# Mixer of a hybrid decoder layer: TensorE in program order with level steps woven into projections, and modulation columns summed by rows

## The chip, the cores and the metric

The kernel runs on one core of one Trainium2 chip. The metric is the time of one execution on the device in microseconds (us); the kernel before takes 2466.71 us, the median of three runs (2466.24 to 2473.23). The engines are TensorE (PE in the rows; PEld is its weight load), VectorE (DVE), ScalarE (ACT), GpSimd (POOL) and SyncE (SP, which issues most DMAs).

## What is computed

One layer for one sequence of T = 2048 tokens and D = 1024 channels, in float32:

```python
mod = silu(c) @ ada_w + ada_b                      # 6 x 1024 columns: shift, scale, gate, twice
h = rms_norm(x, mix_norm_g) * (1 + scale_m) + shift_m
proj = h @ w_in + b_in
q_a, k_a, v_a, q_h, f_h, i_h, g_h = split(proj)    # 512, 128, 128, 512, 512, 512, 512 columns
attn = rms_norm(window_attention(q_a, k_a, v_a, sinks), attn_out_g)
f = lb + (1 - lb) * sigmoid(f_h)                   # recurrence, 4 heads of 128:
#   S_t = diag(f_t) S_(t-1) + (1 - f_t) i_t^T ;  o_t = S_t^T silu(q_h)_t
rec = rms_norm(o, hgrn_out_g) * silu(g_h)
x = x + gate_m * (concat(attn, rec) @ w_out)
# then a gated MLP with a causal convolution of width 3 and the second shift, scale and gate, and a last rms_norm
```

The first half, up to `w_out`, is the mixer; the change lies in it.

## The kernel before, in words

**Tiling.** The mixer works through four groups `g` of 512 tokens (`GT`), each of four blocks of 128. A group's normalised input lies as two float32r parts, `hhi` and `hlo`, by eight slices `k` of 128 channels. Weights are loaded (`..r`), and split into a high part (`..h`, on ACT) and a low part (`..l`, on DVE or POOL). A projection is 24 matmuls into one PSUM bank: for each `k` high by high, low by high and high by low (`mm3`, line 187). The program's names: `hq`, `hf` are the recurrence's query and forget logits of a head, `ps_i` its values (192 matmuls of 256 columns, two weight halves `i 0` and `i 1`), `qp`/`ps_q`, `k`, `v` the attention's, `hg` the output gate.

**The recurrence** goes by heads in pairs (0,1) and (2,3). `hg_q` and `hg_f` evict the projections (`a_q`, `f`, and `K` = 1 - f). `hg_scores` (line 781) prepares both heads on DVE (products `raw`, split into `ph` on ACT and `pl` on POOL; `a_q` and `K` scaled by running products `tot`), and then does ten **level** matmuls (names `lv`, w = 4 to 64, both heads in turn), each reading `a_q` and `K`. After each level `scaled` updates `a_q` and `K` for the next, and DVE puts the result into the score tile `AT` by a predicated copy (ACT does so for w = 32 and 64). Six **sums** with a matrix of ones follow (`lv_d`, 1 and 2, three of each head; the last takes two copies), and two transposes `ktp` of K. `hg_state` (line 886) makes the state (`U`, `mid`, `car`) and the outputs `ho`.

**PSUM banks** are in pools: `mm` 3 (projections), `hg` 2 (levels, sums, ktp, U, ho), `at` 2, `tp` 1. A matmul waits until the bank it is to fill has been emptied.

**Order.** A scheduler orders each engine's instructions unless the engine is pinned to program order (lines 36 to 63). In the mixer's main loop (lines 935 to 984) only ACT is pinned, in parts; TensorE and DVE are placed by the scheduler.

```python
            weights(g, "i", 0, ahead=1)
            pin(True, S)
            hg_scores((0, 1))
            i_tok = proj_i()
            hg_state((0, 1))
```

**Modulation.** 40 column blocks of the modulation are made, of which 24 (16 to 39) are deferred into the group loop: `after()` (line 592) does one at six places of each group through `mod_part` (line 207): one load of 1024 x 128 (512 KB), one multiply by the condition over 128 x 1024, and three additions that halve it. There is one buffer (`ada`, bufs=1). After four blocks `mod_cols_of` sums over partitions with TensorE.

Of the kernel before, what the change touches and what calls it, by code (L numbers as in the profile page):

```python
# [53 lines left out]
def kernel(ctx, tc, x, c, ada_w, ada_b, mix_norm_g, w_in, b_in, attn_sinks, attn_out_g,  # L54
# [175 lines left out]
    with ExitStack() as mx:  # L230
# [103 lines left out]
        for g in range(NG):  # L334
# [254 lines left out]
        for g in range(NG):  # L589
            hhi, hlo = hh  # L590

            def after():

                if defer:
                    t = defer.pop(0)
                    if t % 4 == 0:
# [10 lines left out]
            def proj_i():  # L607
                i_tok = mt.tile([P, BPG, 512], F32, tag="i_tok", bufs=1, name=f"itok_{g}")
                for pp in range(2):
                    ws = weights(g, "i", pp)  # L610
                    for bp in range(2):
                        ps = bank(f"ps_i{g}_{pp}_{bp}", "mm").rearrange("p (a b) -> p a b", a=2)
                        for bb in range(2):
                            b = 2 * bp + bb
                            bs = slice(b * P, (b + 1) * P)
                            for k in range(KT):
                                wh, wl = (t[:, k % 4, :] for t in ws[k // 4])
                                mm3(ps[:, bb, :], hhi[:, k, bs], hlo[:, k, bs], wh, wl, k == 0, k == KT - 1)
                        cs = slice(pp * 256, (pp + 1) * 256)
                        V.tensor_tensor(out=i_tok[:, 2 * bp:2 * bp + 2, cs], in0=ps,  # L620
                                        in1=bi_bc[:, cs].unsqueeze(1).broadcast_to([P, 2, 256]), op=ALU.add)
                return i_tok

            def proj_attn():


                ps = proj(weights(g, "k", 0), f"ps_k{g}")
# [14 lines left out]
                qT = []  # L642
                for pp in range(2):
                    ws = weights(g, "qp", pp)
                    for jj in range(2):
                        j = 2 * pp + jj
                        ps = proj(ws[jj], f"ps_q{g}_{j}")
                        pair = [qa.tile([P, GT], F32R, tag=f"q{j}{e}", name=f"q_{g}_{j}{e}") for e in range(2)]
                        for e in range(2):
                            hp = slice(e * 64, e * 64 + 64)  # L650
                            S.activation(pair[e][hp, :], ps[hp, :], AF.Identity, bias=col("qb", j)[hp, :])
# [913 lines left out]
```

## Time and profile before

| | us |
|---|---|
| median of three runs | 2466.71 (2466.24 to 2473.23) |
| the profiled execution | 2456.9 |
| its span, first to last instruction | 2455.1 |
| TensorE busy (11521 matmul records) | 2296.7, 94% |
| VectorE busy | 1903.9, 78% |
| ScalarE busy | 971.7, 40% |
| GpSimd busy | 917.9, 37% |
| mean granted TensorE clock | 0.973 |

The mixer takes the first 960 us or so of the span, the output projection and the MLP the rest. The busy shares are means over both; the rows below are read by stretches. In a row of the timeline the figure in brackets is the idle time of that engine just before the instruction, with what ended it. A matmul's duration holds the engine's whole pipeline, so from start to start it is shorter than the duration shown. The granted clock is given as a share of the upper level of 2.4 GHz; 0.50 is the lower level of 1.2 GHz.

### The profile page before, as it was taken

The page shows a single profiled execution, that of the slowest core. Times are in us where ns is not written, and L with a number is a line of the kernel's source. Part 1 is how long each engine was busy: PE and PEld are TensorE (multiplying, and loading weights), DVE is VectorE, ACT ScalarE, POOL GpSimd, SP SyncE. Part 2 cuts the span into 40 slices and gives each one's busy share as a digit, 9 for nine tenths or more (in the row PEclk, how much of TensorE's full clock was granted, in tenths as well). Part 3 has the DMA queues.
Part 4 walks back from the last instruction along what each step waited for, and adds up shares of the span by engine and source line. Part 5 has one row for each costly group of instructions (what it writes and reads, how often), then busy time and mean ns, then how long its engine had stood idle before and what let it go on. Part 6 is the DMA issues. An engine that isn't in the chain of part 4 may idle for free.

```text
span 2455.1 us, 31438 instructions
## 1 busy us (share of the span) xinstructions
PE 2296.7 (94%) x11521; PEld 1908.9 (78%) x11521; DVE 1903.9 (78%) x2737; ACT 971.7 (40%) x1658; POOL 917.9 (37%) x760
## 2 busy tenths in 40 slices
PE   5889898998999899999999999899999988999997
PEld 4777786887778778887888888788888776777886
DVE  8888778888876877468888888877888687676766
ACT  3336523723652364455333333433333243323322
POOL 6222212213221221033665664588888710110000
PEclk8999999999999999999999999999999999999999
DMA  8343223223222238574433444654544587777453
GB/s 216 91 121 91 90 69 112 87 81 101 86 87 61 78 120 269 169 244 142 146 123 122 137 130 133 192 164 154 176 158 143 164 278 205 210 188 210 184 215 116
DMA packets 335445, 359.74 MB, mean 147 GB/s; under 512 B 12405, under 2 KB 279371, under 8 KB 335291
## 3 DMA queue, kind: packets, MB, share of 16 engines
q1 hardware_dynamic: 320315, 301.36, 38.8%
q0 software_dynamic: 14976, 56.37, 8.4%
q8 instruction: 91, 1.49, 0.2%
q14 instruction: 63, 0.52, 0.1%
HBM read 250.19 MB, written 107.49 MB: 146 GB/s over the span
## 4 chain that ended last, share of the span: by engine, by line
PE 66%; DVE 13%; DMA 8%; issue 7%; POOL 3%; ACT 2%; SPq 0%; DVEq 0%; POOLq 0%; ACTq 0%
PE ps_u L46 28%; PE ps_d L46 10%; PE ps_o L46 6%; PE lv L46 3%; PE ps_hg L46 3%; PE ps_hq L46 2%; PE ps_hf L46 2%; PE ps_i L46 2%; PE att_o L46 2%; DVE ada L46 2%; DMA Sp<-in_w_down_dram 2%; DMA ada<-in_ada_w_dram 2%; PE ps_q L46 1%; DVE AT L46 1%; DVE raw L46 1%
## 5 line engine op out<-in xcount | busy, mean ns | idle before, releaser
L46 ACT ACTIVATE Th<-da 128x896 fp32r<-128x896 f32 x88 | 83.9, 953 | 230.7 <-PE ps_d L46 210.7
L46 DVE SCALAR_TENSOR_TENSOR cc<-ub,cols,cc 128x1024 f32<-128x1024 f32 x88 | 153.2, 1741 | 14.2 <-ACT cc L46 12.0
L46 DVE TENSOR_TENSOR Tl<-da,Th 128x896 fp32r<-128x896 f32 x88 | 97.1, 1111 | 73.0 <-ACT Th L46 72.7
L46 PE MATMUL lv<-a_q,K 128*128 128x128 f32 (+2 forms) x768 | 80.3, 265 | 42.1 <-DVE K L46 40.0
L46 POOL DMA_DIRECT2D x_d<-o x32 | 27.2, 858 | 237.0 <-DVE o L46 237.0
L46 PEld LDWEIGHTS lv<-a_q,K 128*128 128x128 f32 (+2 forms) x768 | 71.9, 176 | 54.8 <-DVE K L46 28.5
L46 POOL TENSOR_TENSOR s<-wu_0r,s 128x512 f32<-128x512 f32 x44 | 59.2, 1345 | 107.3 <-DVE ws_0l L46 14.7
L46 DVE TENSOR_TENSOR cc<-cc,v 128x1024 f32<-128x1024 f32 x44 | 63.1, 1433 | 43.4 <-ACT cc L46 43.4
L46 POOL TENSOR_TENSOR s<-wu_1r 128x512 f32<-128x512 f32 x44 | 70.6, 1605 | 69.6 <-DVE t_T4l L46 15.7
L46 POOL MEMSET AT<- 128x512 f32 x16 | 8.5, 533 | 233.2 <-PE ho L46 210.4
L46 ACT ACTIVATE cc<-cc 128x1024 f32<-128x1024 f32 x44 | 46.7, 1061 | 121.3 <-DVE cc L46 121.3
L46 POOL TENSOR_TENSOR wu_1r<-wu_0r,wu_1r 128x512 f32<-128x512 f32 x44 | 92.4, 2099 | 3.1
L46 POOL TENSOR_TENSOR pl<-raw,ph 128x512 fp32r<-128x512 f32 x32 | 44.8, 1401 | 101.2 <-ACT ph L46 101.2
L46 POOL TENSOR_SCALAR rv_d<-ssd 128x2 f32<-128x2 f32 x8 | 5.1, 637 | 184.5 <-ACT dx L46 184.5
L46 POOL TENSOR_TENSOR s<-s,wu_0r 128x512 f32<-128x512 f32 x44 | 73.7, 1674 | 0.0
L46 DVE TENSOR_TENSOR v<-ps_u,v 128x512 f32<-128x512 f32 x88 | 60.4, 686 | 15.5 <-PE ps_u L46 12.0
L46 DVE COPY_PREDICATED AT<-lev,lv 128x512 f32<-128x512 uint32 (+1 forms) x96 | 70.1, 730 | 2.4 <-PE lv L46 1.2
L46 DVE TENSOR_TENSOR ada<-ada,cond 128x1024 f32<-128x1024 f32 (+1 forms) x37 | 52.7, 1424 | 16.4 <-DMA ada<-in_ada_w_dram 16.3
L46 ACT ACTIVATE cc<-ub,cols 128x1024 f32<-128x1024 f32 x44 | 54.6, 1240 | 26.3 <-DVE ub L46 26.3
L46 DVE TENSOR_TENSOR a_q<-a_q,tot 128x256 f32<-128x256 f32 x96 | 52.4, 546 | 12.5 <-PE lv L46 11.5
L46 DVE TENSOR_TENSOR o<-ps_d,u 128x512 f32<-128x512 f32 x72 | 49.2, 684 | 15.4 <-ACT u L46 13.9
L46 DVE TENSOR_TENSOR ub<-ps_u,u 128x512 f32<-128x512 f32 x88 | 60.0, 682 | 0.1
(2114 smaller groups left out, 8561.5 us busy)
## 6 DMA issues: line engine op xcount, KB each, us to landing
da<-act_d SPq DMA_DIRECT2D x88, 448.0 KB, 5.8
wu_0r<-in_w_up_dram SPq DMA_DIRECT2D x44, 512.0 KB, 4.4
wu_1r<-in_w_up_dram SPq DMA_DIRECT2D x44, 512.0 KB, 4.4
act_d<-cc POOLq DMA_DIRECT2D x42, 512.0 KB, 4.2
ada<-in_ada_w_dram SPq DMA_DIRECT2D x40, 512.0 KB, 5.9
x_d<-o POOLq DMA_DIRECT2D x32, 512.0 KB, 6.5
act_d<-sm POOLq DMA_DIRECT2D x21, 768.0 KB, 4.1
x<-in_x_dram SPq DMA_DIRECT2D x26, 512.0 KB, 5.6
```

The source lines that it names most:

```text
L46: ins = fn(*args, **kwargs)
```

## The change

**TensorE's order.** TensorE is pinned with ACT from a group's first `hq` projection to the end of the pair (2,3). The projections become generators that yield after each quarter (six matmuls; twelve of 256 columns in `ps_i`), and `weave` runs one step of a recurrence generator, then one piece of the projections:

```diff
+            def weave(gen, *fill):
+                rest = (i for one in fill for i in one)
+                for _ in gen:
+                    next(rest, None)
+                for _ in rest:
+                    pass
```

`hg_scores` yields after every level, sum and transpose (18 steps); the preparation is taken out of it as `hg_prep(h)`, one head at a time. The body of a group becomes:

```diff
+            pin(True, S, TE)
...
+                run(steps_h(hg_q, 0, "hq"), steps_h(hg_f, 0, "hf"), steps_h(hg_q, 1, "hq"))
+                hg_prep(0)
+                run(steps_h(hg_f, 1, "hf"))
+            hg_prep(1)
+            run(steps_i(0), steps(lambda: weights(g, "k", 0), f"ps_k{g}", take_k))
+            q2 = [] if g == 0 else [steps_h(hg_q, 2, "hq")]
+            weave(hg_scores((0, 1)), steps_i(1), *q2)
+            weave(hg_state((0, 1)), steps_h(hg_f, 2, "hf"))
+            mod_step()
+            hg_prep(2)
+            run(steps_h(hg_q, 3, "hq"), steps_h(hg_f, 3, "hf"))
+            mod_step()
+            hg_prep(3)
+            run(steps_q(0), steps_q(1))
+            mod_step()
+            weave(hg_scores((2, 3)), steps_q(2), steps_q(3))
+            mod_step()
+            weave(hg_state((2, 3)), steps(lambda: weights(g, "v", 0), f"ps_v{g}", take_v))
+            pin(False, S, TE)
```

So `weave` of the levels has 8 pieces (`i 1`) in the first pair of the first group, 12 (`i 1` and `hq` 2) in the other pairs (0,1), and 8 (`q` 2 and 3) in the pairs (2,3). The load of the k weights moves from behind `hf` 3 to between `i 0` and `i 1`.

**Modulation by rows.** The 24 column blocks become 48 steps: a part of 512 columns has eight row blocks of 128 x 512 (256 KB), each multiplied by one scalar per partition and added to the part, with two buffers; one step stands at four places of a group and one in each of the eight units of attention. DVE is not pinned and the steps may run ahead of their place.

```diff
-        V.tensor_tensor(out=raw, in0=raw, in1=cond.unsqueeze(2).broadcast_to([P, KT, P]), op=ALU.mult)
-        for n in (4, 2):
-            V.tensor_tensor(out=raw[:, 0:n, :], in0=raw[:, 0:n, :], in1=raw[:, n:2 * n, :], op=ALU.add)
-        V.tensor_tensor(out=to[:, t % 4, :], in0=raw[:, 0, :], in1=raw[:, 1, :], op=ALU.add)
...
+                raw = mt2.tile([P, 4 * P], F32, tag="ada", bufs=2, name=f"ada_{n}_{k}")
+                SY.dma_start(out=raw, in_=ada_v[:, k, 16 * P + n * 4 * P:16 * P + (n + 1) * 4 * P])
...
+            if k == 0:
+                V.tensor_scalar(out=acc_, in0=raw, scalar1=cond[:, 0:1], scalar2=None, op0=ALU.mult)
+            else:
+                V.scalar_tensor_tensor(out=acc_, in0=raw, scalar=cond[:, k:k + 1], in1=acc_, op0=ALU.mult, op1=ALU.add)
+            if k == KT - 1:
+                mod_cols_of(16 + 4 * n, mpart[0])
```

On DVE the eight steps of the first part stand within the two preparations of the first group, and those of two other parts nearly in a row near the ends of groups 1 and 3.

**What stands where: TensorE at the first pair of group 1.** In the names the first number is the group, then the head, then w; a row that stands for several matmuls ends in x4. Before:

```order
L46 MATMUL ps_i1_0_1_3013<-w1_i_0_1l_2675,hhi_1_2520 128x256
L46 MATMUL lv_1_0_4_2806<-a_q1_0_2625,K_1_0_2664 128x128 x4
L46 MATMUL lv_1_1_4_2816<-a_q1_1_2703,K_1_1_2748 128x128 x4
L46 MATMUL ps_i1_0_1_3013<-w1_i_0_1h_2674,hlo_1_2521 128x256
...
L46 MATMUL ps_i1_0_1_3013<-w1_i_0_0h_2668,hhi_1_2520 128x256
L46 MATMUL lv_1_0_8_2826<-a_q1_0_2625,K_1_0_2664 128x128 x4
L46 MATMUL ps_i1_0_1_3013<-w1_i_0_0l_2669,hhi_1_2520 128x256
...
L46 MATMUL lv_1_1_8_2836<-a_q1_1_2703,K_1_1_2748 128x128 x4
```

After:

```order
L46 MATMUL ps_i1_0_1_2865<-w1_i_0_1h_2677,hlo_1_2523 128x256
L46 MATMUL ps_k1_2921<-hhi_1_2522,w1_k_0h_2741 128x512
...
L46 MATMUL ps_k1_2921<-hhi_1_2522,w1_k_0l_2742 128x512
L46 MATMUL lv_1_0_4_2956<-a_q1_0_2628,K_1_0_2667 128x128 x4
L46 MATMUL ps_i1_1_0_2972<-w1_i_1_0h_2805,hhi_1_2522 128x256
...
L46 MATMUL ps_i1_1_0_2972<-w1_i_1_0h_2805,hlo_1_2523 128x256
L46 MATMUL lv_1_1_4_2985<-a_q1_1_2706,K_1_1_2773 128x128 x4
L46 MATMUL ps_i1_1_0_2972<-w1_i_1_1h_2811,hhi_1_2522 128x256
...
L46 MATMUL ps_i1_1_0_2972<-w1_i_1_1h_2811,hlo_1_2523 128x256
L46 MATMUL lv_1_0_8_3007<-a_q1_0_2628,K_1_0_2667 128x128 x4
```

Before, the levels of both heads stand among single matmuls of `ps_i`'s first half; now the first half and all of `ps_k` stand ahead of the first level, and twelve matmuls of the second half stand between one level and the next.

**ACT in the first group**, from the last query eviction on. Before:

```order
L46 ACTIVATE w0_i_1_1h_749<-w0_i_1_1r_747 128x1024
L46 ACTIVATE ph0_0_0_756<-raw0_0_0_761 128x512
L46 ACTIVATE p1_0_0_760<-raw1_0_0_766 128x256
L46 ACTIVATE ph0_0_1_771<-raw0_0_1_776 128x512
L46 ACTIVATE p1_0_1_775<-raw1_0_1_781 128x256
L46 ACTIVATE ph1_0_0_757<-raw2_0_0_789 128x512
L46 ACTIVATE ph1_0_1_772<-raw2_0_1_797 128x512
L46 ACTIVATE AT_0_0_753<-lv_0_0_32_869 32x4x32 x2
L46 ACTIVATE AT_0_1_754<-lv_0_1_32_884 32x4x32 x2
```

After:

```order
L46 ACTIVATE a_q0_2_767<-ps0_4_198,cols_137 128x512
L46 ACTIVATE s_q0_2_769<-ps0_4_198,cols_137 128x512
L46 ACTIVATE ph0_0_1_774<-raw0_0_1_779 128x512
L46 ACTIVATE p1_0_1_778<-raw1_0_1_784 128x256
L46 ACTIVATE ph1_0_1_775<-raw2_0_1_792 128x512
L46 ACTIVATE w0_k_0h_802<-w0_k_0r_800 128x1024
L46 ACTIVATE w0_i_1_0h_808<-w0_i_1_0r_806 128x1024
L46 ACTIVATE w0_i_1_1h_814<-w0_i_1_1r_812 128x1024
...
L46 ACTIVATE kd0_703<-ps_k0_924,cols_137 64x512 x2
```

Before, a weight half of `i` is split ahead of the preparations' splits and k's weights come much later; now k's weights are split behind `ph1` of head 1, and k's own evictions (kd) follow.

**TensorE at the end of pair (2,3) in group 1**: sums and transposes. Before (between the rows shown stand matmuls of `ps_q`):

```order
L46 MATMUL lv_1_2_d_3598<-ph0_1_2_3435,ones_r_694 128x512
L46 MATMUL lv_1_2_d_3598<-pl0_1_2_3437,ones_r_694 128x512
...
L46 MATMUL lv_1_2_1_3602<-p1_1_2_3439,ones_r_694 128x256 x2
...
L46 MATMUL lv_1_2_2_3606<-ph1_1_2_3436,ones_r_694 128x512
L46 MATMUL lv_1_2_2_3606<-pl1_1_2_3438,ones_r_694 128x512
...
L46 MATMUL lv_1_3_d_3611<-ph0_1_3_3450,ones_r_694 128x512
L46 MATMUL lv_1_3_d_3611<-pl0_1_3_3452,ones_r_694 128x512
...
L46 MATMUL lv_1_3_1_3615<-p1_1_3_3454,ones_r_694 128x256 x2
...
L46 MATMUL lv_1_3_2_3619<-ph1_1_3_3451,ones_r_694 128x512
L46 MATMUL lv_1_3_2_3619<-pl1_1_3_3453,ones_r_694 128x512
...
L46 MATMUL ktp_1_2_3624<-ident_127,K_1_2_3303 128x128 x4
...
L46 MATMUL ktp_1_3_3631<-ident_127,K_1_3_3406 128x128 x4
```

After, with no projection from the last levels to the state:

```order
L46 MATMUL ps_q1_3_3658<-hhi_1_2522,w1_qp_1_1l_3424 128x512
L46 MATMUL lv_1_2_64_3729<-a_q1_2_3211,K_1_2_3340 64x64 x4
L46 MATMUL lv_1_3_64_3739<-a_q1_3_3416,K_1_3_3467 64x64 x4
L46 MATMUL lv_1_2_d_3749<-ph0_1_2_3347,ones_r_694 128x512
L46 MATMUL lv_1_2_d_3749<-pl0_1_2_3349,ones_r_694 128x512
L46 MATMUL lv_1_2_1_3753<-p1_1_2_3351,ones_r_694 128x256 x2
L46 MATMUL lv_1_2_2_3757<-ph1_1_2_3348,ones_r_694 128x512
L46 MATMUL lv_1_2_2_3757<-pl1_1_2_3350,ones_r_694 128x512
L46 MATMUL lv_1_3_d_3762<-ph0_1_3_3474,ones_r_694 128x512
...
L46 MATMUL ktp_1_2_3775<-ident_127,K_1_2_3340 128x128 x4
L46 MATMUL ktp_1_3_3782<-ident_127,K_1_3_3467 128x128 x4
...
L46 MATMUL U_1_2_3798<-itok_1_2596,KT_1_2_3780 128x128 x4
```

What stood between the sums, pieces of `ps_q`, now stands ahead of them, and the sums follow each other on the two `hg` banks.

## Rows read from the trace of the kernel before

**Rows 1.** Stretches: length, then busy us of PE, PEld, DVE, ACT, POOL; clock, DMA share, GB/s

```profile
100.00:200.00 100.00, 90.28 (x567) 76.12 (x568) 88.55 (x168) 31.39 (x55) 22.61 (x18) 0.94 0.31 90
...
960.00:1060.00 100.00, 100.00 (x479) 82.80 (x478) 51.87 (x74) 46.08 (x112) 14.68 (x23) 1.00 0.60 203
```

**Rows 2.** PE groups, 0 to 960 us: shape, count | busy us, mean ns | idle before, releasers

```profile
L46 PE MATMUL lv<-a_q,K 128*128 128x128 f32 x384 | 62.7, 321 | 42.1 <-DVE K L46 40.0 <-DVE AT L46 2.2
...
L46 PE MATMUL U<-itok,KT 128*128 128x128 f32 x128 | 16.1, 279 | 2.9 <-DVE AT L46 2.9
...
L46 PE MATMUL ktp<-ident,K 128*128 128x128 f32 x64 | 10.2, 281 | 1.4 <-DVE AT L46 1.3
```

**Rows 3.** PE timeline, first and last wait for K: start, us, instruction, [idle before <-releaser]

```profile
172.64 3.78 PE L46 MATMUL lv<-a_q,K 128*128 128x128 f32 x16 [6.38 <-DVE K L46]
...
820.26 3.76 PE L46 MATMUL lv<-a_q,K 128*128 128x128 f32 x16 [7.42 <-DVE K L46]
```

**Rows 4.** Timelines of DVE (two rows) and POOL (one) before the first of these waits

```profile
165.68 1.22 DVE L46 TENSOR_TENSOR ada<-ada,cond 128x1024 f32<-128x1024 f32 x1 [2.31 <-DMA ada<-in_ada_w_dram]
...
170.16 1.48 DVE L46 TENSOR_TENSOR a_q<-a_q,tot 128x256 f32<-128x256 f32 x1
...
169.92 1.44 POOL L46 TENSOR_TENSOR pl<-raw,ph 128x512 fp32r<-128x512 f32 x1
```

**Rows 5.** The last of seven half-clock stretches behind the waits, and the seven's sum

```profile
815.20:825.40 10.20, 5.14 (x20) 4.88 (x21) 9.07 (x18) 4.21 (x7) 4.62 (x4) 0.50 0.57 155
...
sum 44.20, PE 29.38 PEld 28.96 DVE 39.40 ACT 11.74 POOL 20.15; mean PE 4.20 PEld 4.14 DVE 5.63 ACT 1.68 POOL 2.88
```

**Rows 6.** First group: PE and ACT timelines, and POOL's group of k's low halves

```profile
82.77 0.28 PE L46 MATMUL ps_i<-w_i_0l,hhi 128*128 128x256 f32 x1
82.89 0.28 PE L46 MATMUL ps_i<-w_i_0h,hlo 128*128 128x256 f32 x1
...
100.37 0.58 PE L46 MATMUL ps_i<-w_i_1l,hhi 128*128 128x256 f32 x1 [4.49 <-DVE w_i_1l L46]
...
92.92 1.06 ACT L46 ACTIVATE w_i_1h<-w_i_1r 128x1024 fp32r<-128x1024 f32 x1 [6.96 <-PE ps_i L46]
...
102.89 0.63 ACT L46 ACTIVATE ph<-raw 128x512 fp32r<-128x512 f32 x1 [0.98 <-DVE raw L46]
...
L46 POOL TENSOR_TENSOR w_k_0l<-w_k_0r,w_k_0h 128x1024 fp32r<-128x1024 f32 x4 | 10.2, 2550 | 11.5 <-ACT w_k_0h L46 11.5
```

**Rows 7.** DVE groups, 60 to 960 us

```profile
L46 DVE TENSOR_TENSOR a_q<-a_q,tot 128x256 f32<-128x256 f32 x96 | 52.4, 546 | 12.5 <-PE lv L46 11.5
...
L46 DVE COPY_PREDICATED AT<-lev,lv 128x256 f32<-128x256 uint32 x48 | 35.1, 731 | 2.4 <-PE lv L46 1.2
...
L46 DVE TENSOR_TENSOR ada<-ada,cond 128x1024 f32<-128x1024 f32 x26 | 33.4, 1286 | 16.0 <-DMA ada<-in_ada_w_dram 15.9
...
L46 DVE TENSOR_TENSOR raw<-a_q,K 128x512 f32<-128x512 f32 x32 | 29.5, 921 | 0.0
...
L46 DVE SCALAR_TENSOR_TENSOR q<-ps_q,cols,q 64x512 fp32r<-64x512 f32 x32 | 24.0, 750 | 1.0
...
L46 DVE TENSOR_TENSOR hlo<-hf_h,hhi 128x512 fp32r<-128x512 f32 x28 | 18.6, 686 | 2.2 <-ACT hhi L46 2.0
...
L46 DVE CAST hhi<-hf_h 128x512 fp32r<-128x512 f32 x24 | 9.9, 423 | 3.9 <-ACT hf_h L46 3.8
```

**Rows 8.** PE timeline at another wait, and the stretch behind it

```profile
644.39 0.50 PE L46 MATMUL sc<-kd,q 128*128 128x256 f32 x1 [2.92 <-DVE comb L46]
...
644.50:647.90 3.40, 3.40 (x13) 3.01 (x14) 3.40 (x11) 2.31 (x7) 1.65 (x2) 0.50 0.36 109
```

**Rows 9.** DMA issues, 60 to 900 us (two rows), whole run (one): KB, us to landing

```profile
ada<-in_ada_w_dram SPq DMA_DIRECT2D x24, 512.0 KB, 3.8
...
w_qp_0r<-in_w_in_dram SPq DMA_DIRECT2D x16, 256.0 KB, 3.6
...
ada<-in_ada_w_dram SPq DMA_DIRECT2D x40, 512.0 KB, 5.9
```

More of the change, by code (lines that the diff above doesn't have):

```diff
@@ L605, in proj @@
                 return ps
[L607 to L622, printed above, removed]
@@ L624, in proj_attn, with steps, steps_i @@
-            def proj_attn():
-                ps = proj(weights(g, "k", 0), f"ps_k{g}")
+            def steps(w, name, fn):
+                w, ps = w(), bank(name, "mm")
+                for k in range(KT):
+                    mm3(ps, w[0][:, k, :], w[1][:, k, :], hhi[:, k, :], hlo[:, k, :], k == 0, k == KT - 1)
+                    if k % 2 and k < KT - 1:
+                        yield
+                fn(ps)
+                yield
+            def steps_i(pp):
+                ws = weights(g, "i", pp)
+                for bp in range(2):
+                    ps = bank(f"ps_i{g}_{pp}_{bp}", "mm").rearrange("p (a b) -> p a b", a=2)
+                    for bb in range(2):
+                        b = 2 * bp + bb
+                        bs = slice(b * P, (b + 1) * P)
+                        for k in range(KT):
+                            wh, wl = (t[:, k % 4, :] for t in ws[k // 4])
+                            mm3(ps[:, bb, :], hhi[:, k, bs], hlo[:, k, bs], wh, wl, k == 0, k == KT - 1)
+                            if k == 3 or k == KT - 1 and bb == 0:
+                                yield
+                    cs = slice(pp * 256, (pp + 1) * 256)
+                    V.tensor_tensor(out=i_tok[:, 2 * bp:2 * bp + 2, cs], in0=ps,
+                                    in1=bi_bc[:, cs].unsqueeze(1).broadcast_to([P, 2, 256]), op=ALU.add)
+                    yield
@@ L641, in proj_attn @@
                                            in1=kd[e][hp, P:].bitcast(F32), op0=ALU.add, op1=ALU.subtract)
[L642 to L651, printed above, removed]
-                        for e in range(2):
-                            hp = slice(e * 64, e * 64 + 64)
-                            op = slice(64 - e * 64, 128 - e * 64)
-                            V.scalar_tensor_tensor(out=pair[e][op, :], in0=ps[hp, :], scalar=col("qb", j)[hp, :],
-                                                   in1=pair[e][hp, :].bitcast(F32), op0=ALU.add, op1=ALU.subtract)
-                        qT.append(pair)
@@ L658, in proj_attn, with take_q @@
-                ps = proj(weights(g, "v", 0), f"ps_v{g}")
+            qT, vts = [], []
+            def take_q(ps):
+                j = len(qT)
+                pair = [qa.tile([P, GT], F32R, tag=f"q{j}{e}", name=f"q_{g}_{j}{e}") for e in range(2)]
+                for e in range(2):
+                    hp = slice(e * 64, e * 64 + 64)
+                    S.activation(pair[e][hp, :], ps[hp, :], AF.Identity, bias=col("qb", j)[hp, :])
+                for e in range(2):
+                    hp = slice(e * 64, e * 64 + 64)
+                    op = slice(64 - e * 64, 128 - e * 64)
+                    V.scalar_tensor_tensor(out=pair[e][op, :], in0=ps[hp, :], scalar=col("qb", j)[hp, :],
+                                           in1=pair[e][hp, :].bitcast(F32), op0=ALU.add, op1=ALU.subtract)
+                qT.append(pair)
@@ L843, in hg_scores @@
-                for h in hs_:
-                    scaled(h, 2)
                 w = 4
```

177 lines of the change are left out of this document (88 added, 89 removed).

## Prediction

> **What bounds the kernel now.** I read the busy time and clock by 100-us stretches first [rows 1]. From 960 to 1060 us, past the mixer, TensorE is busy 100.00 of 100 us; in the mixer, of which 100 to 200 us is one stretch, it is busy 90.28 of 100 at a clock of 0.94, with VectorE (DVE) at 88.55. So TensorE sets the end, closely followed by DVE in the mixer, and what is to be had lies in the mixer's idle spots and in the half-clock stretches behind them. All rows after about the third block of the output projection stand in one order in both kernels, so the change acts only in the first 960 us or so.
>
> Next, TensorE by groups [rows 2]: of all its waits from 0 to 960 us the first level matmuls of a recurrence pair carry by far the most, 42.1 us, of which 40.0 wait for K, the last tile of the pair's preparation on DVE. The timeline shows them one by one [rows 3]: the first and the last of the seven are given, 6.38 and 7.42 us; the seven are 40.0 together, one in each pair but the first. Why K is late is seen on DVE and GpSimd (POOL) just before the first of them [rows 4, 7]: a modulation load that DVE waits for stands in its row (2.31 us idle, then 1.22 busy), and an a_q step that costs 0.546 on average takes 1.48 beside a POOL subtraction. TensorE meanwhile has run out of projections that the scheduler let it do early.
>
> Each such wait is paid twice: behind it the granted clock is 0.50, which is the 1.2 GHz level, for 3.4 us or more, 10.2 behind the last [rows 5]. In the seven stretches TensorE was busy 29.38 us; at the upper level (2.4 GHz) the same work takes half, so **14.7 us** are lost there.
>
> **The change part by part.** The sum is made against the profiled execution, 2456.9 us; the median of the three timed runs, 2466.71, lies 9.8 above it, and I add those 9.8 at the end.
>
> A. **Preparation ahead, other projections between.** A pair's DVE preparation now starts when its own projections are evicted, and TensorE has, up to the first level, ps_i's first half and k for pair (0,1), or hq, hf, q0 and q1 for pair (2,3). A matmul of 256 columns starts 0.12 us after the one before [rows 6], so one of 512 is 0.24 and a projection of 24 is 5.8 us; four are 23. A head's preparation is eleven DVE instructions of at most 0.92 us [rows 7], so two heads take under 20. K is ready before TensorE asks for it, in all seven: **-40.0**. With no wait there, the half-clock stretch goes: **-14.7**. The bound for both on the other side is rival 4.
>
> B. **First group.** There the first level did not wait, but ps_i did, for the low half of its weights: 4.49 us [rows 6]. Now k stands behind ps_i's first half, and the split of k's weights stands in ACT's pinned order behind ph1 of head 1, which needs the last DVE product of both preparations, with eight modulation steps between. By the rows of before: the second matmul of ps_i starts at 82.77, and 96 matmuls of 0.12 end near 94.0. The last ph starts at 102.89 and takes 0.63, the weight split 1.06, POOL's low half 2.55: 107.1. That is 13.1 us idle where 4.49 stood: +8.6. DVE gets two weight splits less ahead of it and more modulation; I take **+8**, with 4 (product 3 us sooner, nothing ahead on POOL) and 13 (POOL's other halves ahead) as ends. The low clock behind it was there before too and cancels.
>
> C. **Unfilled ends.** A pair has 18 steps (10 levels, 6 sums, 2 transposes), but the fill has 8 pieces in pairs (2,3) and in the first pair, 12 in the other pairs (0,1). From there on, sums follow each other with only two PSUM banks (hg), which DVE must empty. A head's sums take TensorE 0.48 + 0.24 + 0.48 = 1.2 us, and DVE four copies of 0.731 [rows 7], 2.92. For a pair (2,3): 5.84 - 2.4 = 3.4 us, plus the two q evictions of 0.750 that the last fill leaves ahead of them, less the two banks that are free at the start (1.46): 3.5 us, four times, 14.0. For pairs (0,1) with 12 pieces six copies are left: 4.4 - 1.7 - 1.46 = 1.2, three times, 3.6. First pair: 3.4 + 0.7 (one eviction of ps_i) - 1.46 = 2.7. Together 20.3. The waits for AT that stand there now go into it: 2.2, 1.3 and 2.9 [rows 2], 6.4. Net **+13.9**, between 0 (DVE keeps up) and 20. Does the clock fall behind them? A wait of 2.92 us did bring it to 0.50 [rows 8], and 3.40 us of work then ran at half; the nearest value for 3.5 is that one: 1.7 us lost, four times, **+6.8**, between 0 and 14.
>
> D. **First projection of the next group.** Before, hq and hf of head 0 and hq of head 1 were mixed by k, so TensorE had work while DVE made hhi and hlo. Now hq of head 0 stands alone in order. One k needs 0.423 + 0.686 = 1.11 us of DVE [rows 7] against 0.72 of three matmuls: 0.39 each, 3.1 for eight. The transposes between fill part; I take 2.2 in each of three groups, **+6.6**, between 0 and 9.3.
>
> E. **Modulation.** Twenty-four blocks had a multiply of 1.286 us each and three additions; 48 steps now have one instruction each. No such instruction of 512 columns with both inputs in SBUF is in the trace as a fused form; bounds are 0.750 (the q eviction) and 0.921 (the raw product), and I take the first, to whose kind it belongs: 48 x 0.750 = 36 us against 31 for the multiplies alone. DVE saves about the additions. It is not on the path once A holds, so **0** on the time, from -5 to the cost in rival 3. The loads are twice as many and half as big. Loads of 512 KB landed after 3.8 us and of 256 KB after 3.6 [rows 9]: halving buys nearly nothing in time to land. The Trainium skill speaks against this split: DMA: Bandwidth & Descriptors, section Anatomy of one DMA, gives a fixed cost of about 2 us to a transfer whatever its size, for the GpSimd path (these are issued by SyncE); by its fit 256 KB would be an estimated 2.6 us and 512 KB 3.2, and the two rows, 3.6 and 3.8, agree in direction. The sum is the same by either.
>
> Everything else (attention, output gates, the waits of 1 to 2 us between groups) keeps its work and I leave it. Sum: -40.0 - 14.7 + 8 + 13.9 + 6.8 + 6.6 = -19.4, so 2437.5 for a profiled execution and **2447** for the median.
>
> **The rivals.**
>
> 1. *The ends cost nothing.* DVE has slack after A and empties banks in time: C adds nothing over today's 6.4, no clock falls, D is filled by transposes, B is 4. -54.7 + 4 = -50.7: 2416. For it: DVE is rid of the additions. Against: four copies per head are 2.9 us against 1.2 of TensorE whatever stands ahead.
>
> 2. *DVE is slower at the ends.* The last a_q and K steps of a pair, two of each, stand ahead of the copies. If POOL is at weights' halves then, each can take 1.48 as in [rows 4] instead of 0.55: 3.7 us per pair, whole in four pairs (2,3) (14.9), half in the three with 12 pieces (5.6). -19.4 + 20.5 = +1: 2468, no change. Against: over the whole mixer the mean is 0.546, so most are not hit. The Trainium skill has this as an exclusive lock: SBUF — State Buffer, section SBUF: two separate sides, says that DVE with two SBUF inputs and a GpSimd operation that reads SBUF block each other for a whole instruction. By that rule the trace's 1.48 is such a case, and the copies, which read PSUM, are not held up.
>
> 3. *Modulation loads hold DVE, and the kernel is slower.* There are two buffers, and in three places (first preparation, ends of groups 1 and 3) all eight steps of a part stand nearly in a row on DVE. Eight steps with two buffers last at least four times load plus step: 4 x (3.6 + 0.75) = 17.4 us, of which DVE fills about 80% with its other work [rows 1], 14 us. The remaining 3.4 are less in sum than the 16.0 that DVE waits on such loads today [rows 7]. But the load's median over the whole run is 5.9 us [rows 9]; with that a burst lasts 26.6, DVE stands 12.6, and TensorE, in order behind the evictions, stands with it: 3 x 12.6 = 38, 2447 + 38 = 2485. It makes the kernel slower by over 0.3% from a load of about 5.1 us on. Against: 3.8 is the median in this stretch.
>
> 4. *The change doesn't do what it says in pairs (2,3).* If their preparation is still late, because attention's q weights and evictions are in DVE's row ahead of it, four of the seven waits stay, about 27 of the 40 us, and about 8 of the clock's: -19.4 + 35 = +16: 2482. Against: 23 us of projections against under 20 of DVE.
>
> **How the numbers follow.** Forecast 0.50 (2447, alone 2434 to 2461), rival 1 0.18, rival 2 0.15, rival 3 0.11, rival 4 0.06. A measurement of this kernel can tell about 0.3% from no change, 7.4 us: faster is below 2459.3, slower above 2474.1. Forecast and rival 1 are faster, rival 2 is the same, rivals 3 and 4 are slower: 0.68, 0.15, 0.17. The range reaches down to rival 1's 2416 and up to 2480, which leaves rivals 3 and 4 mostly outside, and a little below: 2 in 10.
>
> **What would show it.** A: in the changed trace no level matmul waits over 1 us for K, and the seven 0.50 stretches are gone; level waits for K in pairs (2,3) would show rival 4. B: ps_k of the first group waits about 13 us for its low weights, from ACT or POOL. C: the sums and transposes at a pair's end wait for AT, some 20 us in all, and four short 0.50 stretches follow. D: hq of head 0 waits for hlo or hhi, some 7 us. E: DVE's idle time behind the modulation loads stays under 16 us; if it is 30 or more in three places, rival 3 holds. I am wrong first if C's ends are much longer than 3.5 us, or if TensorE in order waits at a place that had none before.

## The result and the profile after

The changed kernel takes 2491.85 us (median of four runs, 2489.86 to 2496.37) against 2466.47 for the kernel before: a ratio of 1.0101, 95% interval 1.0077 to 1.0126. It is 25 us **slower**; the prediction was 2447, 19 us faster.

Where the time went is seen by one stretch in each kernel, from the first matmul of `ps_i` to the first of `ps_o`, which holds nearly the same TensorE work in both. Columns: length, then busy us of PE, PEld, DVE, ACT, POOL with their records, clock, DMA share, GB/s. First before:

```profile
82.55:913.76 831.21, 760.83 (x4836) 659.68 (x4837) 672.88 (x1361) 377.27 (x836) 202.68 (x196) 0.96 0.30 89
```

and after:

```profile
82.68:936.13 853.45, 774.04 (x4844) 664.39 (x4845) 662.26 (x1315) 385.09 (x841) 191.21 (x196) 0.95 0.29 86
```

The stretch is 22.2 us longer, and that is two things. TensorE's idle time (length less busy) went from 70.4 to 79.4 us: +9.0. And TensorE's **busy** time went from 760.8 to 774.0: +13.2, with eight records more of 4836 to do; the same matmuls ran for longer at the lower clock. Behind the stretch, where both kernels have one order but for its first blocks, the profiled executions differ by 11 us more (1541 against 1552). The timed medians differ by 25, not 33 (the profiled execution before lay 9.8 under its median), and in the other kernels below with TensorE pinned the same end takes anything from 1544 to 1557, so I do not put those 11 down to the change.

TensorE's groups after, to be held against [rows 2] and [rows 6]; columns as there:

```profile
L46 PE MATMUL lv<-a_q,K 128*128 128x128 f32 x384 | 52.9, 282 | 15.4 <-DVE K L46 8.8 <-DVE AT L46 6.6
...
L46 PE MATMUL ps_k<-hhi,w_k_0h 128*128 128x512 f32 x32 | 13.6, 426 | 11.9 <-ACT w_k_0h L46 11.9
...
L46 PE MATMUL att_t<-ident,osb 128*128 128x128 f32 x63 | 10.2, 286 | 8.9 <-DVE osb L46 8.7 <-DVE st L46 0.2
...
L46 PE MATMUL lv<-ph,ones_r 128*128 128x512 f32 x16 | 8.7, 542 | 8.0 <-DVE AT L46 7.7
...
L46 PE MATMUL ktp<-ident,K 128*128 128x128 f32 x64 | 15.1, 381 | 6.6 <-DVE AT L46 6.6
...
L46 PE MATMUL lv<-p,ones_r 128*128 128x256 f32 x32 | 8.2, 344 | 6.6 <-DVE AT L46 6.6
L46 PE MATMUL lv_d<-ph,ones_r 128*128 128x512 f32 x16 | 7.9, 497 | 3.8 <-ACT AT L46 3.2 <-DVE AT L46 0.4
...
L46 PE MATMUL lv<-a_q,K 128*32 128x32 f32 x256 | 7.1, 198 | 2.8 <-DVE AT L46 2.8
...
L46 PE MATMUL ps_k<-hhi,w_k_0l 128*128 128x512 f32 x32 | 13.5, 422 | 2.1 <-POOL w_k_0l L46 2.1
...
L46 PE MATMUL ps_hq<-hlo,w_hq_0h 128*128 128x512 f32 x24 | 9.7, 404 | 2.1 <-DVE hlo L46 2.1
```

The waits for K fell from 40.0 to 8.8 us, as the change means to do. What stands in their place: k of the first group 11.9 + 2.1 (before, 4.49 on `ps_i`); at the pairs' ends 8.0, 6.6, 6.6 and 3.8 for the sums and transposes; levels that wait for AT, 6.6 and 2.8 where 2.2 stood; and `att_t` at the passage to the next group, 8.9.

Single waits on the timeline of TensorE after (start, us, instruction, idle before):

```profile
610.94 1.06 PE L46 MATMUL lv<-a_q,K 128*128 128x128 f32 x8
...
615.40 0.98 PE L46 MATMUL lv<-a_q,K 128*128 128x128 f32 x4 [2.02 <-DVE K L46]
...
857.28 0.50 PE L46 MATMUL lv<-ph,ones_r 128*128 128x512 f32 x1 [1.69 <-DVE AT L46]
...
859.80 0.77 PE L46 MATMUL lv<-p,ones_r 128*128 128x256 f32 x2 [0.46 <-DVE AT L46]
...
720.05 1.11 PE L46 MATMUL att_t<-ident,osb 128*128 128x128 f32 x4 [3.65 <-DVE osb L46]
```

The first row is the first level of head 2, in group 2, which does not wait. The second is what is left of [rows 3]: 2.02 us for K at the first level of the pair's second head, once in each pair (2,3) (2.73 in the first group). The next two are at the end of a pair: 1.69 and 0.46, each for a copy into AT. At the pairs' ends none is as long as the waits before. But look at the clock there, in the same columns as the first rows, for the ends of the four pairs (2,3):

```profile
209.20:217.70 8.50, 7.01 (x28) 5.79 (x29) 4.87 (x8) 2.25 (x3) 0.00 (x0) 0.60 0.00 0
423.40:435.30 11.90, 10.28 (x40) 8.36 (x40) 7.87 (x14) 2.25 (x3) 0.00 (x0) 0.57 0.15 46
639.30:651.20 11.90, 10.75 (x40) 7.97 (x40) 6.98 (x12) 2.25 (x3) 0.00 (x0) 0.57 0.02 5
856.90:872.20 15.30, 13.68 (x49) 10.89 (x50) 9.07 (x21) 2.25 (x3) 0.00 (x0) 0.55 0.22 67
```

In these stretches of 8.5 to 15.3 us the granted clock is 0.55 to 0.60, that is the 1.2 GHz level for 6.8 to 13.7 us of each, although TensorE was busy most of the time and no single wait exceeded 1.7 us. Before, a half-clock stretch stood behind one long wait [rows 5]; now it stands around many short ones. The Trainium skill has such a case on the page TensorE: Matmul & The Clock Gate, section A second HAM failure mode: psum-queue depth-cycling: TensorE idles briefly between groups of matmuls, often enough that the clock oscillates. These rows agree with it: waits of 1.7 us at most, and a clock of 0.55 to 0.60.

### The profile page after: what moved, and what is told of

Same layout as the page of the kernel before. It is cut to its first block, busy times and chain, and to the rows that moved or that the text cites. A ratio compares the mean times of both kernels' runs of the same rounds, so it can differ in the third digit from the quotient of the medians.

```text
span 2488.1 us, 31372 instructions
## 1 busy us (share of the span) xinstructions
PE 2315.5 (93%) x11521; PEld 1915.2 (77%) x11521; DVE 1894.4 (76%) x2689; ACT 977.9 (39%) x1662; POOL 905.2 (36%) x760
## 4 chain that ended last, share of the span: by engine, by line
PE 39%; POOL 11%; issue 8%; DVE 6%; DMA 6%; ACT 1%; SPq 0%; DVEq 0%; POOLq 0%; ACTq 0%
PE ps_u L46 16%; PE ps_d L46 10%; PE ps_o L46 6%; POOL s L46 3%; DMA Sp<-in_w_down_dram 2%; POOL sm L46 2%; POOL wu_1r L46 2%; POOL ct_1r L46 2%; POOL ct_0r L46 1%; PE ps_i L46 1%; PE ps_hf L46 1%; PE ps_hg L46 1%; DMA wu_1r<-in_w_up_dram 1%; PE ps_hq L46 1%; DMA cw_0r<-in_w_down_dram 1%
## 5 line engine op out<-in xcount | busy, mean ns | idle before, releaser
L46 POOL TENSOR_TENSOR s<-wu_0r,s 128x512 f32<-128x512 f32 x44 | 59.4, 1351 | 107.3 <-DVE ws_0l L46 14.8
L46 POOL TENSOR_TENSOR a_q<-a_q,s_q 128x512 f32<-128x512 f32 x16 | 23.1, 1444 | 175.7 <-ACT s_q L46 175.7
L46 PEld LDWEIGHTS lv<-a_q,K 128*128 128x128 f32 (+2 forms) x768 | 63.0, 158 | 31.0 <-issue 23.9
L46 PE MATMUL lv<-a_q,K 128*128 128x128 f32 (+2 forms) x768 | 69.8, 245 | 18.1 <-DVE AT L46 9.3
L46 DVE COPY_PREDICATED AT<-lev,lv 128x512 f32<-128x512 uint32 (+1 forms) x96 | 70.2, 731 | 10.8 <-PE lv L46 8.6
L46 ACT ACTIVATE cc<-ub,cols 128x1024 f32<-128x1024 f32 x44 | 54.6, 1240 | 26.7 <-DVE ub L46 26.3
L46 DVE TENSOR_TENSOR a_q<-a_q,tot 128x256 f32<-128x256 f32 x96 | 43.3, 453 | 19.7 <-PE lv L46 19.2
```

The lines of the kernel that those rows point to most:

```text
L46: ins = fn(*args, **kwargs)
```

## The experiments

Theory: the loss sits in TensorE's fixed order, by waits at the pairs' ends and the clock that falls with them. Rivals: the modulation by rows costs it; the new sequence of the code costs it, pinned or not; DVE sets the pace and waits only move. Each experiment ran beside the kernel before on the same chip, and ratios are against it.

**Modulation alone.**

In the kernel before, each of the six places makes two row steps, with two buffers, in place of one column block:

```diff
             def after():
...
-                    mod_part(t, mt2.tile([P, KT, P], F32, tag="ada", bufs=1, name=f"ada_{t}"), part[-1][1])
+                mod_step()
+                mod_step()
```

> The kernel before with the modulation by rows alone (two steps at each of its six places per group, two buffers); TensorE and the recurrence as before. Theory order (the loss of 25 us sits in TensorE's fixed order: k's wait in the first group, the pairs' ends, the half clock behind them): no change or a small gain, 2455 to 2470 us, waits for K between 30 and 45 us as before. Rival modulation (twice as many loads and the steps in DVE's row cost it): slower than before by 10 us or more, 2477 and up.

Measured: 2458.63 against 2467.36, ratio 0.9965 (0.9954 to 0.9977). A gain of 9 us; K still makes TensorE wait, 30.6 us where it was 40.0:

```profile
L46 PE MATMUL lv<-a_q,K 128*128 128x128 f32 x384 | 61.6, 318 | 33.2 <-DVE K L46 30.6 <-DVE AT L46 2.4
```

The modulation is not the cause of the loss; it helps by itself.

**The new order with the old modulation.**

In the changed kernel, the column blocks with one buffer are put back at six places of a group, as in:

```diff
-            mod_step()
+            after()
             hg_prep(2)
```

> The changed kernel with the modulation by column blocks put back (six blocks per group, one buffer). Theory order: as slow as the changed kernel or slower, 2488 to 2510 us, since DVE has some 26 us more. Rival modulation: back near the kernel before, 2460 to 2475 us.

Measured: 2497.89, ratio 1.0114 (1.0097 to 1.0131), as slow as the changed kernel (the intervals overlap). So the loss is the new order's; whether the sequence or the pin makes it is left to the run with TensorE free.

**k's weights split early in the first group.**

```diff
                 hg_f(0, ps0[2])
+                weights(g, "i", 0, ahead=1)
                 hg_prep(0)
```

> The changed kernel with one line more: in the first group the weights of i and k are asked for, and so split on ScalarE, ahead of the first preparation. Theory order: the wait of ps_k in the first group falls from 13.9 us to under 4 and with it part of the half clock there: 8 to 12 us faster than the changed kernel, 2479 to 2484. If the wait only moves to the first level matmul behind it (K late), the gain is under 4 us.

Measured: 2487.65, ratio 1.0078 (1.0061 to 1.0096), which overlaps the changed kernel's interval. The wait of `ps_k` is gone, but i's second half waits in its place (TensorE's timeline):

```profile
108.24 0.58 PE L46 MATMUL ps_i<-w_i_0h,hhi 128*128 128x256 f32 x1 [7.10 <-ACT w_i_0h L46]
...
110.56 0.58 PE L46 MATMUL ps_i<-w_i_0l,hhi 128*128 128x256 f32 x1 [1.74 <-DVE w_i_0l L46]
```

So 13.9 us became 7.1 + 1.7, and the gain is not clear of noise.

**TensorE free, all else as changed.**

```diff
-            pin(True, S, TE)
+            pin(True, S)
```

> The changed kernel with ScalarE pinned as it is and TensorE left to the scheduler. Theory order: the scheduler puts projections between the sums again, waits for AT at the ends fall from 33 us to under 15, and the time lies 10 to 30 us under the changed kernel, 2460 to 2480. If it is the code's new sequence (preparation by head, k ahead, six-matmul pieces) and not the pin that costs, it stays within 5 us of the changed kernel.

Measured: 2443.16, ratio 0.9907 (0.9891 to 0.9924): 24 us **faster** than the kernel before and 49 faster than the changed one, by one word. Here the scheduler puts the last attention work behind the first `ps_o`, so the whole executions are compared: span and busy time from the page of the changed kernel,

```profile
span 2488.1 us, 31372 instructions
...
PE 2315.5 (93%) x11521; PEld 1915.2 (77%) x11521; DVE 1894.4 (76%) x2689; ACT 977.9 (39%) x1662; POOL 905.2 (36%) x760
```

and of this one:

```profile
span 2447.9 us, 31378 instructions
...
PE 2300.1 (94%) x11521; PEld 1897.9 (78%) x11521; DVE 1893.4 (77%) x2689; ACT 977.9 (40%) x1663; POOL 908.6 (37%) x760
```

The span is 40.2 us shorter: idle 147.8 in place of 172.6 (-24.8), and busy 15.4 less for the same 11521 records, the clock. (The medians are 49 apart: the profiled execution here is the slowest of its kernel, that of the changed kernel the fastest.) Its stretch up to `ps_o`, for a later comparison, three groups of TensorE, and its longest wait for K:

```profile
82.93:887.37 804.44, 752.29 (x4785) 641.30 (x4785) 653.46 (x1300) 381.31 (x830) 197.16 (x194) 0.97 0.30 91
...
L46 PE MATMUL lv<-a_q,K 128*128 128x128 f32 x384 | 53.2, 282 | 26.6 <-DVE K L46 18.4 <-DVE AT L46 8.2
...
L46 PE MATMUL ktp<-ident,K 128*128 128x128 f32 x64 | 10.3, 283 | 3.0 <-DVE AT L46 3.0
...
L46 PE MATMUL lv<-p,ones_r 128*128 128x256 f32 x32 | 7.1, 304 | 2.2 <-DVE AT L46 1.9
...
107.16 0.77 PE L46 MATMUL lv<-a_q,K 128*128 128x128 f32 x2 [11.39 <-DVE K L46]
```

K is waited for more here than with TensorE pinned (18.4 us against 8.8), but 11.39 of it is one wait in the first group, where the pinned kernel waited 13.9 for k's weights; in the pairs (2,3) the waits are 7.0 against 8.8, nearly the same. The levels wait for AT nearly as long as with the pin, 8.2 against 9.4. What falls is the waiting at the ends: `ktp` from 6.6 to 3.0, and the sums from 18.4 in all to the 2.2 of the third row.

**TensorE free in the woven stretches only.**

```diff
+            pin(False, TE)
             weave(hg_scores((0, 1)), steps_i(1), *q2)
             weave(hg_state((0, 1)), steps_h(hg_f, 2, "hf"))
+            pin(True, TE)
...
+            pin(False, TE)
             weave(hg_scores((2, 3)), steps_q(2), steps_q(3))
```

> The changed kernel with TensorE pinned only outside the woven stretches (levels, sums and states are left to the scheduler). Theory ends: most of the 48 us between pinned and free TensorE come back, 2445 to 2462, the waits for AT fall by half. If the pin costs elsewhere (projections in strict order, the passage between groups and attention), it stays above 2475.

Measured: 2452.81, ratio 0.9947 (0.9931 to 0.9963). Span and busy time from its page:

```profile
span 2448.4 us, 31378 instructions
...
PE 2299.8 (94%) x11521; PEld 1898.8 (78%) x11521; DVE 1896.1 (77%) x2689; ACT 978.7 (40%) x1663; POOL 905.7 (37%) x760
```

39 of the 49 us in the medians come back with the levels, sums and states alone; idle is 148.6 and busy 2299.8, as in the free kernel. The remaining 10 us belong to what is still pinned, the projections and the passage. Where in them is not shown: the two profiled executions, one the fastest but one of seven and the other the slowest of six, differ by 0.5 us.

**Idle matmuls at the ends**, to part the clock from the waits. After each recurrence step that has no piece left, two matmuls that nothing reads run on a spare bank:

```diff
+                pad = bank(f"pad{g}_{len(pads)}", "at")
...
                 for _ in gen:
-                    next(rest, None)
+                    if next(rest, 0) == 0:
+                        for _ in range(2):
+                            TE.matmul(pad, lhsT=hhi[:, 0, 0:P], rhs=hhi[:, 0, :], start=True, stop=True)
```

> The changed kernel with two idle matmuls of 512 columns (0.24 us each, result never read) after each recurrence step that has no piece of a projection left: 68 places, 33 us of extra TensorE work in the stretches where it waits some 33 us for AT. Theory clock (the short waits at the ends cost twice, since the clock falls behind them: 36 us of mixer work at half, 18 of it behind the ends of pairs (2,3)): the half-clock loss falls to under 20 and the kernel gets faster by 5 us or more, under 2487. Theory chain (the ends are bound by DVE's copies alone, and the clock is a by-product): not faster, 2490 to 2510, with the padding's work on top.

Measured: 2478.27, ratio 1.006 (1.0037 to 1.0082). The interval still overlaps the changed kernel's at its edge; the medians are 13.6 us apart, in the direction of the clock theory. The trace is clearer: the mixer stretch, the end of the last pair, the added matmuls, and the sum over all stretches of the mixer at the lower clock:

```profile
83.10:928.92 845.82, 786.60 (x4981) 676.91 (x4981) 663.29 (x1315) 385.56 (x841) 190.21 (x196) 0.97 0.29 87
...
843.00:860.00 17.00, 15.19 (x107) 10.86 (x107) 14.09 (x27) 3.79 (x9) 0.00 (x0) 1.00 0.11 32
...
L46 PE MATMUL pad<-hhi 128*128 128x512 f32 x136 | 45.0, 412 | 0.0
...
sum 47.79, PE 33.65 PEld 28.24 DVE 40.47 ACT 20.06 POOL 18.35; mean PE 4.21 PEld 3.53 DVE 5.06 ACT 2.51 POOL 2.29
```

At that end the clock is now 1.00 (and at the three before it). TensorE's busy time in the stretch rose to 786.6, but 136 added matmuls at 0.24 us from start to start are 33 of it; the kernel's own work took about 754 where it took 774. The last row agrees: 33.65 us of TensorE's work ran at the lower level, 69.60 in the changed kernel, and half of that difference is 18.0 us. So 18 to 20 us of busy time were the clock's, and with 33 us of useless work the stretch became 7.6 us shorter.

**More fill for pairs (2,3).**

```diff
-            run(steps_q(0), steps_q(1))
+            run(steps_q(0))
...
-            weave(hg_scores((2, 3)), steps_q(2), steps_q(3))
+            weave(hg_scores((2, 3)), steps_q(1), steps_q(2), steps_q(3))
```

> The changed kernel with q1 moved into the weave of pair (2,3): 12 pieces in place of 8 for 18 steps, and the first level 5.8 us earlier. If the ends lack fill: the waits for AT in pairs (2,3) fall by a third or more, 5 to 12 us faster than the changed kernel. If DVE sets the pace of the whole stretch: the waits move to K at the first level (8.8 now, 20 or more then) and the time stays within 5 us of the changed kernel.

Measured: 2519.11, ratio 1.022 (1.0191 to 1.0249): 27 us slower than the changed kernel, worse than either theory said. The wait at the second head's first level grew (now for `tot`, the last tile of the preparation), and the sums wait nearly as much as before:

```profile
402.29 2.05 PE L46 MATMUL lv<-a_q,K 128*128 128x128 f32 x8 [7.57 <-DVE tot L46]
...
L46 PE MATMUL lv<-a_q,K 128*128 128x128 f32 x384 | 55.1, 290 | 31.8 <-DVE tot L46 31.8
...
L46 PE MATMUL lv<-ph,ones_r 128*128 128x512 f32 x16 | 7.8, 488 | 8.5 <-DVE AT L46 8.1
...
L46 PE MATMUL lv<-a_q,K 128*32 128x32 f32 x256 | 7.7, 206 | 10.8 <-DVE AT L46 10.3
```

Four waits of 7.6 to 9.1 us where 2.0 to 2.7 stood. So DVE's preparation was only just late with 23 us of projections ahead, and taking 5.8 of them away shows in full. The ends did not gain from the four pieces: the sums wait 16.2 us in all (18.4 in the changed kernel), `ktp` 7.5 (6.6), and the levels of w = 32, the last row, 10.8 where 2.8 stood.

**TensorE pinned from the fourth projection on**, so that the passage from attention is free:

```diff
-            pin(True, S, TE)
+            pin(True, S)
...
                 run(steps_h(hg_q, 0, "hq"), steps_h(hg_f, 0, "hf"), steps_h(hg_q, 1, "hq"))
+                pin(True, TE)
                 hg_prep(0)
                 run(steps_h(hg_f, 1, "hf"))
+            pin(True, TE)
```

> The changed kernel with TensorE pinned only from hf of head 1 on (the first three projections of a group left to the scheduler). By step D of the prediction (6.6 us) and by the two kernels with free weaves and wholly free (10 us apart, 5 of it between attention and ps_i): 4 to 8 us faster than the changed kernel, 2484 to 2488. If the passage between groups costs nothing: no change from 2492.

Measured: 2477.22, ratio 1.0035 (1.0023 to 1.0047): 15 us under the changed kernel, twice what was expected.

```profile
82.98:925.95 842.97, 768.38 (x4844) 658.86 (x4845) 662.92 (x1315) 385.15 (x841) 191.61 (x196) 0.96 0.29 87
...
L46 PE MATMUL att_t<-ident,osb 128*128 128x128 f32 x64 | 10.1, 282 | 1.9 <-DVE osb L46 1.6 <-DVE st L46 0.2
```

`att_t` waits 1.9 us in place of 8.9, and the stretch's busy time falls by 5.7 with it, idle by 4.8. The 6.6 us of the expectation were the waits for `hhi` and `hlo` alone, without `att_t` and without the clock.

**TensorE free with the old modulation.**

> The changed kernel with TensorE left to the scheduler and the modulation by column blocks put back. If the two parts add up: by the run of modulation alone (-8.7 us against before) and by the changed kernel with the old modulation (+6 against the changed one), this is 6 to 10 us slower than the free kernel with the modulation by rows, 2449 to 2454, and still 13 us or more under before. If the gain of the free kernel is the modulation's alone, it is back at 2465.

(The edit is that of the second experiment and that of the free kernel together.) Measured: 2476.03, ratio 1.003 (1.0012 to 1.0048): 33 us slower than with the modulation by rows, where 6 to 10 were expected.

```profile
82.54:917.55 835.01, 767.07 (x4777) 653.67 (x4777) 686.90 (x1343) 374.45 (x825) 195.30 (x194) 0.96 0.29 87
...
L46 PE MATMUL lv<-a_q,K 128*128 128x128 f32 x384 | 56.5, 293 | 34.1 <-DVE AT L46 17.1 <-DVE K L46 16.7 <-ACT f L46 0.2
```

The first row is the stretch up to `ps_o`, which stands beside that of the free kernel above. DVE is busy 686.9 us in the stretch, 33.4 more than in the free kernel, and the stretch is 30.6 longer: TensorE idles 15.8 us more and is busy 14.8 more. So the parts do not add up: the modulation is worth 9 us in the order before, about 6 (not clear of noise) with TensorE pinned, and 33 with TensorE free in the new sequence. Seen the other way, the pin costs 49 us with the modulation by rows, but 22 with the column blocks (2497.89 against 2476.03), and the new sequence, free and with the column blocks, is 8.5 us slower than the kernel before (2467.5 beside it). That DVE sets the pace there is suggested by the levels, which wait 17.1 us for AT where it is 8.2 in the free kernel, but it is not shown: why it costs nearly all of DVE's added time there and so little elsewhere I have not separated further.

**Two attempts at the first group.** The free kernel with k's weights early, and with all weights of the first group early (`weights(g, "i", 0)`, which asks for i's second half too):

> TensorE left to the scheduler, and i's and k's weights of the first group split ahead of the first preparation. If the first group's wait is a cost of its own, it adds its 4 to 8 us to the gain: 2435 to 2440. If the scheduler has covered it already, no change from 2443.

> TensorE free, and in the first group the weights of both halves of i and of k split ahead of the preparations (in the kernel before this one i's second half was not, and TensorE waited 7.1 + 0.9 us for it). 4 to 8 us under that one's 2441.7 if the splits do not delay the preparations; no change if the wait moves to K at the first level.

Measured: 2441.72, ratio 0.9902 (0.9876 to 0.9927), and 2443.1, ratio 0.9898 (0.9875 to 0.9921): neither is apart from the free kernel. The pinned kernel with all weights early and the idle matmuls:

> The changed kernel, TensorE pinned, with the idle matmuls at the pairs' ends and all weights of the first group split early: the two costs that pinning showed (half clock behind the ends, first group's wait) taken out at once. Additive: 2478 - 10 = 2466 to 2470, level with the kernel before. What then remains to the free kernel's 2443 are the waits themselves at ends, levels and passages, some 25 us.

Measured: 2475.23, ratio 1.0037 (1.0023 to 1.005), no better than the idle matmuls alone (2478.27, 1.0037 to 1.0082) where 10 us less were expected. The wait of the first group moved on to the first level of the second head:

```profile
111.77 1.62 PE L46 MATMUL lv<-a_q,K 128*128 128x128 f32 x6 [9.60 <-DVE tot L46]
```

9.6 us there, and 6.6 in the free kernel with all weights early. In the free kernel without early weights it was 11.39. So the wait for k's weights covered DVE's preparation behind it: taking it away bought nothing that can be told.

With both edits in it, this last kernel's interval (up to 1.005) is clear of the changed kernel's (from 1.0077).

Pinned with finer pieces (three matmuls), or with the pieces spread over all 18 steps, was not tried, so it is not shown that a fixed order as such must lose. The best that ran are the free kernels, 2442 to 2443 us, 23 to 24 under the kernel before.

## Why the prediction was wrong, step by step

The terms of the sum, for the stretch from `ps_i` to `ps_o`, against what the traces show (us, changed kernel against before):

| | forecast | measured |
|---|---|---|
| A, waits for K | -40.0 | -31.2 |
| B, first group | +8 | +9.4 |
| C, waits for AT at the ends, with those of the levels (7.7 before, 34.4 after) | +13.9 | +26.7 |
| D, passage: `hlo` (+2.1) and `att_t` (+4.5) | +6.6 | +6.6 |
| other idle time | 0 | -2.5 |
| idle time together | -11.5 | +9.0 |
| clock, measured as busy time | -7.9 | +13.2 |
| together | -19.4 | +22.2 |

Two steps failed, by about the same amount: the clock by 21.1 us, and the waits by 20.5, mainly C with the levels (12.8) and A (8.8). Neither gives the sign alone: with the clock as forecast the stretch would have come out at +1.1, and with the waits as forecast at +1.7, both about no change. The rows of before that the table needs and that are not shown yet:

```profile
L46 PE MATMUL att_t<-ident,osb 128*128 128x128 f32 x64 | 10.4, 287 | 4.4 <-DVE osb L46 4.2 <-DVE st L46 0.2
...
L46 PE MATMUL lv<-p,ones_r 128*128 128x256 f32 x32 | 7.1, 305 | 1.2 <-DVE AT L46 1.0
```

**A, waits for K.** Right in mechanism, mis-sized: -31.2 in place of -40.0. The step that failed is "two heads take under 20 us of DVE against 23 of projections": it counted the preparation alone and not what else stands in DVE's row in pairs (2,3). DVE's timeline after, group 2, from the last row of head 2's preparation to the end of head 3's:

```profile
598.35 0.15 DVE L46 TENSOR_TENSOR tot<-tot 128x4 f32<-128x4 f32 x1
598.85 1.37 DVE L46 TENSOR_TENSOR w_qp_0l<-w_qp_0r,w_qp_0h 128x512 fp32r<-128x512 f32 x1 [0.35 <-ACT w_qp_0h L46]
...
606.13 0.69 DVE L46 TENSOR_TENSOR w_qp_1l<-w_qp_0r,w_qp_1h 128x512 fp32r<-128x512 f32 x1 [2.39 <-ACT w_qp_1h L46]
...
607.94 0.54 DVE L46 TENSOR_SCALAR f<-f,omc,lbc 128x512 f32<-128x512 f32 x1
...
614.84 1.82 DVE L46 TENSOR_TENSOR K<-K,tot 128x256 f32<-128x256 f32 x2
```

Between the two preparations stand eight halves of q's weights (the first and one later are shown), 598.85 to 607.94, with 2.39 us of waiting for ACT in them; head 3's preparation starts at 607.94, 8 us after the last matmul of its projection started (599.80), and its K is done at about 615.3 (the first of the two steps in the last row; the second scales head 2 for its next level). TensorE had done its four projections at 610.94, did head 2's first level and one piece, and stood at head 3's until 615.40. So rival 4 held in small, 2.0 to 2.7 us per pair. And the levels' own chain was left out: C took their 2.2 us for AT away, but with six matmuls between levels they wait 9.4, 7.2 more than before. The pin is not the reason: with TensorE free it is 8.2.

**The clock.** The largest single miss. The sum had -14.7 for the seven old stretches and +6.8 for four new ones, -7.9 in all. Measured by the busy time of the same work it is +13.2: 21 us off. The granted clock comes near it. These are the sums over every stretch at the lower level between `ps_i` and `ps_o`, before and after, and over the four at the ends of pairs (2,3) after:

```profile
sum 64.82, PE 46.39 PEld 44.51 DVE 56.29 ACT 18.33 POOL 26.77; mean PE 4.22 PEld 4.05 DVE 5.12 ACT 1.67 POOL 2.43
...
sum 88.74, PE 69.60 PEld 55.54 DVE 58.26 ACT 30.18 POOL 14.50; mean PE 5.80 PEld 4.63 DVE 4.85 ACT 2.51 POOL 1.21
...
sum 40.97, PE 36.33 PEld 29.15 DVE 23.73 ACT 9.00 POOL 0.00; mean PE 9.08 PEld 7.29 DVE 5.93 ACT 2.25 POOL 0.00
```

TensorE did 46.4 us of work at the lower level before and 69.6 after; half of the difference, +11.6, is lost. The four ends have 36.3 of it, so they lost 18.2 us where the sum had 6.8: that term was mis-sized. I gave the clock one stretch of 3.4 us behind each end, from the one row at hand [rows 8], where a single wait of 2.92 us was followed by undisturbed work. At the ends the short waits go on, and so does the low clock, for 6.8 to 13.7 us. The idle matmuls took it away, which shows it.

**B, first group.** +9.4 (13.9 against 4.49) for +8: right, and the cause too (ACT, then POOL). But the experiments show that it was not to be had: behind it DVE's preparation is as late.

**C, unfilled ends.** Waits of sums and transposes after: 8.0 + 6.6 + 6.6 + 3.8 = 25.0, for a forecast of 20.3; the mechanism is as written, about a quarter larger, and part of the waits (3.2) is for ACT's copies of w = 64, which the step did not count.

**D, passage to the next group.** hq waits 2.1 us for `hlo`, not 6.6; but `att_t` waits 8.9 (4.4 before), since in fixed order no projection can fill what the scheduler filled. That the two make 6.6 together is chance. By the run with the pin set later the passage cost 10.5 us of the stretch, half of it busy time, which I put down to the clock. "Everything else keeps its work and I leave it" was the failing sentence here: a pinned engine changes the places next to the pinned ones.

**E and rival 3.** The fused step took 0.779 us on average, near the 0.750 taken, and DVE waited 0.7 us in all for the halved loads, 16.0 before:

```profile
L46 DVE SCALAR_TENSOR_TENSOR part<-ada,cond,part 128x512 f32<-128x512 f32 x42 | 32.7, 779 | 1.1 <-DMA ada<-in_ada_w_dram 0.7 <-DVE ssh L46 0.3
```

So rival 3, which had the right sign, had the wrong mechanism. (By its own numbers the load from which it would have shown is 5.0 us, not 5.1; nothing hangs on it.) The 48 loads landed after a median of 3.0 us. The fixed cost of a transfer that the Trainium skill gives (DMA: Bandwidth & Descriptors, Anatomy of one DMA) did not show in DVE's waits, with two buffers in place of one. E was worth -9 by itself, in the kernel before, where the text had 0: K came earlier there.

**What the sum lacked** as a whole: it priced every wait as if the scheduler's order were kept around it. That order put single matmuls between sums; the pin put pieces of six, and none at the ends. With TensorE free the same code gives 2443, close to the 2447 forecast, but that is luck and no merit of the sum: the terms differ (K is still waited for 18.4 us, and the ends hardly).

## What to carry to other kernels

Before an engine is taken from a scheduler into a fixed order, count the fill at every step of the chain, the last ones above all, and run the same code with the engine free: here that one word was 49 us. A row of waits of 1 to 2 us can cost nearly as much again in clock as in waiting, so price them by how long the row lasts, and read it from the busy time of equal work. When a second engine is nearly as busy (in this stretch VectorE 672.9 and TensorE 760.8 of 831.2 us), a wait that is removed can move, as it did in three runs here; look for what is just as late behind it before it is counted as a gain. Two parts of a change need not add up: run each with and without the other.

## What the runs showed of the hardware

At the ends of pairs (2,3) the clock was at half for up to 13.7 us, with no wait over 1.7 us, and it was full there when 33 us of useless matmuls were put in. The seven long waits of 4 to 7 us before lost 14.7 us by the clock; the short ones at the four ends after lost 18.2. Of the four waits of 2.0 to 2.7 us for K that were left after the change, two had 3.4 us at half clock behind them (from 615.64 and 834.09 us), and two had none.
